# RWKV delta rule in chunks: the triangular inverse applied to strict keys and values ahead of the recursion

## The chip, the cores and the metric

The kernel runs on one core of one Trainium2 chip. The metric is the device time of one execution in microseconds, and the kernel before has a median of 2791.34 us of three runs (2788.96 to 2798.7). All data are fp32; the large matrices are multiplied as split fp32r parts, the small products of the recursion as plain fp32.

## The reference, cut to what matters

The model has two parts: first two hybrid layers (a mixer and an FFN each) on the tokens, then a second block with differential attention and an RWKV branch, both on the same tokens, followed by a PEER mixture of experts. The change is in the RWKV branch. It is a delta rule with decay, run over 256 tokens and 16 heads of 64, forward and over the reversed sequence (axis d):

```python
def wkv_scan(s0, scan_in):
    def step(s, inp):
        w, kk, a, k, v, r = inp
        sa = jnp.einsum('dbhij,dbhj->dbhi', s, kk)
        s = s * w[..., None, :] - sa[..., :, None] * (kk * a)[..., None, :] + v[..., :, None] * k[..., None, :]
        return s, jnp.einsum('dbhij,dbhj->dbhi', s, r)
    return lax.scan(step, s0, scan_in)
...
    s_ctx, y_c = wkv_scan(s0, scan_c)
    _, y_x = wkv_scan(s_ctx, scan_x)
```

It is scanned over the context first (only the state `s_ctx` is wanted), then over x from that state, where the outputs `y` are wanted.

## The kernel before

The scan is cut into 8 chunks of 32 tokens. Within a chunk the delta rule is solved by a 32 x 32 triangular inverse, so that the recursion has 8 steps of matrix products. Heads go in two halves (`hf`) of 8, in 4 tiles of two heads (index m, head b of the pair on partitions 64b to 64b+63). That makes four passes of `wkv_front` (line 1177) and `wkv_back` (line 1354): passes 1 and 2 on the context (src = 0, halves 0 and 1), each issued from `ffn` of layer 0 and 1, and passes 3 and 4 on x (src = 1), issued from `second`. The two directions run together in each pass.

`wkv_front` loads keys and values, normalises, builds decayed keys KB (K and B parts side by side), the strict keys and, for src = 1, the decayed r in WR, and the decay PC of each chunk. Per chunk it multiplies KB by WR (line 1300) and masks: ML holds the strict products, NK the inclusive ones (src = 1). Of ML, the rows 32 to 63 and 96 to 127 go through DRAM (din, lines 1311 to 1316) into Bt; a loop of 31 steps on VectorE (lines 1320 to 1325, tiles X, tmp) forms the inverses, which return through DRAM (dout, lines 1327 to 1332) into ML. Beside that loop, keys are transposed (KT, line 1346) and U = strict times values is formed (line 1353), both per chunk pair and direction, and each copied from PSUM by ScalarE (line 268).

`wkv_back` does per step n, for both directions (chunk n forward, chunk 7 - n backward): product of WR with the state S (line 1376), four sums into U on 32 partitions each (line 1381, recorded as line 274), for src = 1 four copies of the r part into Y, the inverse times U (line 1392) with two copies (line 268), the product with the keys (line 1404), and per direction S + product (line 274) and times the decay PC (line 271). For src = 1 the outputs follow (line 1420) and after them norm, bonus and gate, with a store to od (line 1453).

The Tile scheduler writes the order of each engine's queue before the run; the scan's work has a raised priority, and is woven into the work around it: FFN matmuls in passes 1 and 2, the projections of the second block and its attention in passes 3 and 4. In `ffn` the scan's matmuls have two PSUM banks (shown as m and x) that are taken in turn. In `second` the front has two and the back three. Tiles of 4 KB per partition come from a pool of tag w4 (5 slots in `ffn`, 8 in `second`), those of 8 KB from w8 (6 and 9 slots). A tile waits until the slot that it takes has been let go by its last reader. In pass 4, WR lies in the work tiles hh and hl. The state goes from `ffn` to `second` through DRAM (Sd, line 907).

## Time and profile before

| what | value |
|---|---|
| median of three runs | 2791.34 us (2788.96, 2791.34, 2798.7) |
| profiled execution, its own time | 2798.71 us |
| its span | 2796.9 us |
| TensorE busy | 2635.9 us (94%) |
| VectorE busy | 1978.4 us (71%) |
| ScalarE busy | 1423.3 us (51%) |
| GpSimd busy | 14.2 us, 45 instructions |

Times of the trace count from the span's start. PE is TensorE (PEld its weight load), DVE VectorE, ACT ScalarE, POOL GpSimd, SP the engine that issues DMAs. Tiles are named by the program: w stands for the pools w4 and w8, a, m, x for PSUM banks. A plain fp32 matmul is recorded as two instructions, a transpose against the identity as one. Passes 1 and 2 lie at about 390 to 667 and 1017 to 1263 us, passes 3 and 4 between 1355 and 1835 us; the experts follow.

### The profile page before, as it was taken

What the parts mean: (1) busy time and instruction counts of PE and PEld (TensorE: products, weight loads), DVE (VectorE), ACT (ScalarE), POOL (GpSimd) and SP (SyncE); (2) the same over time, 40 slices, a digit from 0 to 9 for tenths busy, and PEclk for the clock granted to TensorE, in tenths of its full rate; (3) what the DMA queues carried; (4) which work ended last, traced back from release to release, by engine and by line L of the source; (5) the groups of instructions that cost most, each with busy time, mean ns of one, the idle gap of its engine ahead of it and who ended that gap; (6) DMA issues with size and microseconds to landing.
All of it is one profiled execution on the core that took longest, in us unless ns stands there. A gap on an engine that the chain in (4) does not pass through costs nothing.

```text
span 2796.9 us, 54976 instructions
## 1 busy us (share of the span) xinstructions
PE 2635.9 (94%) x21856; PEld 2293.4 (82%) x21856; DVE 1978.4 (71%) x4085; ACT 1423.3 (51%) x2392; POOL 14.2 (1%) x45
## 2 busy tenths in 40 slices
PE   7999899999999999987998979989989999999999
PEld 7986588886997768877888755779989998888887
DVE  5996668765897658766788776566987765666665
ACT  4554446543555446534664655444446554444444
POOL 0000000000000000000000000000000000000000
PEclk9999999999999999988999976699999999999999
DMA  5532866546543555535746522264664346666665
GB/s 189 175 124 88 263 225 199 168 152 219 167 147 126 162 199 170 173 107 166 237 134 200 166 68 59 67 200 163 190 185 137 122 149 208 215 208 219 207 216 183
DMA packets 212433, 472.00 MB, mean 169 GB/s; under 512 B 52816, under 2 KB 86480, under 8 KB 211152
## 3 DMA queue, kind: packets, MB, share of 16 engines
q1 hardware_dynamic: 212176, 468.48, 52.4%
q8 instruction: 172, 2.82, 0.4%
q14 instruction: 85, 0.70, 0.1%
HBM read 427.77 MB, written 40.63 MB: 167 GB/s over the span
## 4 chain that ended last, share of the span: by engine, by line
PE 79%; DVE 10%; DMA 6%; ACT 4%; issue 2%; SPq 0%; DVEq 0%; ACTq 0%
PE a L333 8%; PE a L335 8%; PE a L334 8%; PE b L353 4%; PE b L351 4%; PE b L352 4%; PE b L1767 3%; PE x L335 3%; PE x L333 3%; PE x L334 3%; PE a L352 3%; PE a L351 3%; PE a L353 3%; DVE wl L277 3%; DMA raw<-in_peer 2%
## 5 line engine op out<-in xcount | busy, mean ns | idle before, releaser
L312 ACT ACTIVATE wh<-raw 128x1024 fp32r<-128x1024 f32 (+1 forms) x701 | 638.2, 913 | 689.3 <-PE a L334 247.4
L277 DVE TENSOR_TENSOR wl<-raw,wh 128x1024 fp32r<-128x1024 f32 (+1 forms) x701 | 727.4, 1041 | 357.9 <-ACT wh L312 332.6
L333 PE MATMUL a<-hh,wh 128*128 128x256 f32 x1920 | 550.2, 287 | 8.8 <-ACT hh L1621 4.1
L335 PE MATMUL a<-hh,wl 128*128 128x256 f32 x1920 | 549.5, 286 | 4.5 <-DVE wl L277 4.2
L334 PE MATMUL a<-hl,wh 128*128 128x256 f32 x1920 | 547.2, 285 | 0.6 <-DVE hl L277 0.5
L333 PEld LDWEIGHTS a<-hh,wh 128*128 128x128 f32 x1920 | 365.5, 190 | 22.0 <-ACT wh L312 4.9
L335 PEld LDWEIGHTS a<-hh,wl 128*128 128x128 f32 x1920 | 365.2, 190 | 14.8 <-DVE wl L277 9.0
L334 PEld LDWEIGHTS a<-hl,wh 128*128 128x128 f32 x1920 | 364.9, 190 | 5.4 <-DVE hl L277 0.7
L333 PE MATMUL x<-hh,wh 128*128 128x256 f32 x720 | 205.8, 286 | 5.6 <-ACT wh L312 5.2
L335 PE MATMUL x<-hh,wl 128*128 128x256 f32 x720 | 206.6, 287 | 3.0 <-DVE wl L277 3.0
L334 PE MATMUL x<-hl,wh 128*128 128x256 f32 x720 | 204.9, 285 | 0.0
L352 PE MATMUL b<-wl,ah 128*128 128x512 f32 x512 | 201.0, 393 | 0.0
L351 PE MATMUL b<-wh,ah 128*128 128x512 f32 x512 | 191.2, 393 | 2.8 <-issue 2.8
L353 PE MATMUL b<-wh,al 128*128 128x512 f32 x512 | 191.8, 391 | 0.0
L333 PEld LDWEIGHTS x<-hh,wh 128*128 128x128 f32 x720 | 137.2, 191 | 9.0 <-ACT wh L312 6.7
L335 PEld LDWEIGHTS x<-hh,wl 128*128 128x128 f32 x720 | 136.9, 190 | 5.7 <-DVE wl L277 4.4
L1802 ACT ACTIVATE ah<-pact 128x256 fp32r<-128x256 f32 x128 | 52.6, 412 | 173.1 <-PE b L352 160.3
L334 PEld LDWEIGHTS x<-hl,wh 128*128 128x128 f32 x720 | 137.1, 190 | 0.8
L352 PE MATMUL a<-wl,hh 128*128 128x256 f32 (+2 forms) x416 | 128.6, 309 | 8.0 <-DVE wl L277 7.9
L351 PE MATMUL a<-wh,hh 128*128 128x256 f32 (+2 forms) x416 | 125.3, 308 | 6.2 <-DVE hl L395 3.9
L277 DVE TENSOR_TENSOR wl<-rawv,wh 128x1024 fp32r<-128x1024 f32 x84 | 101.7, 1222 | 37.1 <-ACT wh L312 37.0
L353 PE MATMUL a<-wh,hl 128*128 128x256 f32 (+2 forms) x416 | 125.9, 304 | 0.0
(672 smaller groups left out, 5436.7 us busy)
## 6 DMA issues: line engine op xcount, KB each, us to landing
raw<-in_flat SPq DMA_DIRECT2D x289, 512.0 KB, 4.0
raw<-in_peer SPq DMA_DIRECT2D x172, 512.0 KB, 3.9
raw<-in_flat SPq DMA_DIRECT2D x228, 256.0 KB, 3.6
rawv<-in_peer SPq DMA_DIRECT2D x84, 512.0 KB, 4.6
TG<-in_flat SPq DMA_DIRECT2D x52, 512.0 KB, 5.9
parked<-act SPq DMA_DIRECT2D x89, 128.0 KB, 2.1
pact<-parked SPq DMA_DIRECT2D x89, 128.0 KB, 4.5
w<-vtd SPq DMA_DIRECT2D x32, 128.0 KB, 4.1
```

What stands on the lines that cost most here:

```text
L277: self.nc.vector.tensor_tensor(out, a, b, op=ALU.subtract)
L312: self.nc.scalar.activation(h, src, AF.Copy)
L333: mm(ps, wh[:, k], xh[:, k], start=first and k == 0, stop=False)
L334: mm(ps, wh[:, k], xl[:, k], start=False, stop=False)
L335: mm(ps, wl[:, k], xh[:, k], start=False, stop=last and k == nk - 1)
L351: mm(ps, xh[:, k], wh[:, k], start=first and k == 0, stop=False)
L352: mm(ps, xh[:, k], wl[:, k], start=False, stop=False)
L353: self.last = mm(ps, xl[:, k], wh[:, k], start=False, stop=last and k == nk - 1)
L1767: nc.tensor.matmul(ps[:, c], a[:, n, g, :, c], b[:, g, :, c], start=n == 0, stop=n == 2)
L1802: nc.scalar.activation(ah, act, AF.Copy)
```

## The change

1. S is not cleared at first; in step 0 of a context pass the product with S is left out, and the key product is copied to S.
2. U tiles hold both directions by step: `UV[n % 2][:, n // 2]`. Values are loaded by 16 DMAs of half the size.
3. The strict keys in WR are transposed into four new w4 tiles AT: for src = 0 by 64 products with the identity and 16 copies, for src = 1 by 32 transposes and 8 copies.
4. U = strict times values, and then the inverse times U, are two passes of eight groups each ahead of the recursion (`half in (0, 32)`), apart from the key transposes.
5. alpha, the inverse applied to the strict keys, is formed (128 products, one group of banks per direction), multiplied by the decay of the chunk before and written over the strict keys in WR. For src = 1 GpSimd multiplies the r part likewise.
6. In the recursion, the inverse product with its copies is gone; the sums into U are two masked ones over 128 partitions (`urows`); D = S times decay is formed by GpSimd beside the S product, and S = D + key product. The context passes multiply S by the last decay at the end.

```diff
@@ -902,8 +902,7 @@
             wa = tg[:, :T]
             nc.sync.dma_start(wa, self.wad)
             S = self.t(pool, [128, 2, 4, 64], "S")
-            nc.gpsimd.memset(S, 0.0)
-            self.wkv_back(self.wkv_front(pool, 0, l, self.zc, wa), S)
+            self.wkv_back(pool, self.wkv_front(pool, 0, l, self.zc, wa), S)
             nc.sync.dma_start(self.Sd[l], S)
...
@@ -1304,6 +1303,12 @@
                     if src:
                         self.mul(NK[:, d, q, b], pq[b][:, d, :, 0], incl[:, d].unsqueeze(1).to_broadcast([128, 4, 32]))
+        if src:
+            for d in range(2):
+                now, old = slice(1 - d, 8 - d), slice(d, 7 + d)
+                v = WR[d][:, :, now, 0]
+                nc.gpsimd.tensor_tensor(v, v, PC[:, d, :, old].unsqueeze(3).to_broadcast([128, 4, 7, 32]), op=ALU.mult)
...
@@ -1333,11 +1338,13 @@
         KT = [k.rearrange("p m (q c) x s -> p m q (c x s)", c=2) for k in KB]
-        UV = [self.w8(pool, [128, 4, 4, 128]) for d in range(2)]
-        for d in range(2):
-            for g in range(4):
-                o = UV[d].rearrange("p (t h) m c -> p h t (m c)", h=2)
-                nc.sync.dma_start(o[64 * (g % 2):64 * (g % 2) + 32, g // 2], vtd[32 * g:32 * g + 32])
+        UV = [self.w8(pool, [128, 4, 4, 128]) for e in range(2)]
+        for g in range(4):
+            rows, at = slice(64 * (g % 2), 64 * (g % 2) + 32), slice(32 * g, 32 * g + 32)
+            for t in range(2):
+                for d in range(2):
+                    n = 4 * t + g if d == 0 else 7 - 4 * t - g
+                    nc.sync.dma_start(UV[n % 2][rows, n // 2].rearrange("p m c -> p (m c)"), vtd[at, t])
         for q in range(4):
             for d in range(2):
                 qd = q if d == 0 else 3 - q
@@ -1345,67 +1352,111 @@
                 for m in range(4):
                     nc.tensor.transpose(ps[:, m], KT[d][:, m, qd], self.ident)
                 self.evac(KT[d][:, :, qd], ps)
+        AT = [[self.w4(pool, [128, 2, 4, 128]) for h in range(2)] for d in range(2)]
+        for q in range(4):
+            for d in range(2):
+                at = AT[d][q // 2][:, q % 2]
+                ps = self.bank().rearrange("p (m c) -> p m c", m=4)
+                for m in range(4):
+                    if src:
+                        nc.tensor.transpose(ps[:, m], WR[d][:, m, 2 * q:2 * q + 2].rearrange("p c x s -> p (c x s)"), self.ident)
+                        continue
+                    for c2 in range(2):
+                        mm(ps[64 * c2 + 32:64 * c2 + 64, m], WR[d][:, m, 2 * q + c2, 0], self.ident, start=True, stop=True)
+                if src:
+                    self.evac(at, ps)
+                else:
+                    for c2 in range(2):
+                        u = slice(64 * c2 + 32, 64 * c2 + 64)
+                        self.evac(at[u], ps[u])
+        steps = lambda n: [(d, *divmod(n if d == 0 else 7 - n, 2)) for d in range(2)]
+        for half in (0, 32):
+            for n in range(8):
+                uv = UV[n % 2][:, n // 2]
                 ps = self.bank().rearrange("p (m b i) -> p m b i", m=4, b=2)
                 for m in range(4):
                     for b in range(2):
-                        for c2 in range(2):
-                            R = slice(64 * c2, 64 * c2 + 32)
-                            mm(ps[64 * c2 + 32:64 * c2 + 64, m, b], ML[R, d, qd, b, m], UV[d][R, qd, m, 64 * b:64 * b + 64], start=True, stop=True)
+                        for d, q, c2 in steps(n):
+                            R = slice(64 * c2 + half, 64 * c2 + half + 32)
+                            mm(ps[64 * c2 + 32:64 * c2 + 64, m, b], ML[R, d, q, b, m], uv[R, m, 64 * b:64 * b + 64], start=True, stop=True)
                 for c2 in range(2):
                     u = slice(64 * c2 + 32, 64 * c2 + 64)
-                    self.evac(UV[d][u, qd], ps[u].rearrange("p m b i -> p m (b i)"))
+                    self.evac(uv[u], ps[u].rearrange("p m b i -> p m (b i)"))
+        for d in range(2):
+            pa = [self.bank().rearrange("p (q m s) -> p q m s", q=4, m=4) for c2 in range(2)]
+            for q in range(4):
+                for m in range(4):
+                    for b in range(2):
+                        for c2 in range(2):
+                            u = slice(64 * c2 + 32, 64 * c2 + 64)
+                            mm(pa[c2][64 * b:64 * b + 64, q, m], AT[d][q // 2][u, q % 2, m, 64 * b:64 * b + 64], ML[u, d, q, b, m], start=True, stop=True)
+            for c2 in range(2):
+                al = WR[d][:, :, c2::2, src].rearrange("p m q s -> p q m s")
+                first = 0 if d == 0 else 7
+                if first % 2 != c2:
+                    lo, hi = 0, 4
+                else:
+                    lo, hi = 1 - d, 4 - d
+                    nc.vector.tensor_copy(al[:, first // 2], pa[c2][:, first // 2])
+                old = PC[:, d, :, 2 * lo + c2 + 2 * d - 1:2 * hi + c2 + 2 * d - 2:2].rearrange("p m q -> p q m")
+                self.mul(al[:, lo:hi], pa[c2][:, lo:hi], old.unsqueeze(3).to_broadcast([128, hi - lo, 4, 32]))
         Y = [self.w4(pool, [128, 2, 4, 128]) for d in range(2)] if src else None
-        return src, hf, PC, WR, KT, UV, ML, NK, Y, bond if src else None
-    def wkv_back(self, state, S, od=None):
-        src, hf, PC, WR, KT, UV, ML, NK, Y, bond = state
+        W = [w.rearrange("p m c x s -> p (m c x s)") for w in WR] if src else wc.rearrange("p d m c s -> p (d m c s)")
+        return src, hf, PC, W, KT, UV, NK, Y, bond if src else None
+    def wkv_back(self, pool, state, S, od=None):
+        src, hf, PC, W, KT, UV, NK, Y, bond = state
         nc, P = self.nc, self.P2
         mm = nc.tensor.matmul
         m0 = 4 * hf
-        U64 = [u.rearrange("p q m (b i) -> p q m b i", b=2) for u in UV]
+        U64 = [UV[n % 2][:, n // 2].rearrange("p m (b i) -> p m b i", b=2) for n in range(8)]
         for n in range(8):
             dc = [(d, *divmod(n if d == 0 else 7 - n, 2)) for d in range(2)]
-            pp = [self.bank()[:, 0:256].rearrange("p (m i) -> p m i", m=4) for b in range(2)]
-            for m in range(4):
-                for d, q, c2 in dc:
-                    rows = slice(64 * c2, 64 * c2 + 64) if src else slice(64 * c2 + 32, 64 * c2 + 64)
-                    for b in range(2):
-                        Q = slice(64 * b, 64 * b + 64)
-                        mm(pp[b][rows, m], WR[d][Q, m, 2 * q + c2].rearrange("p x s -> p (x s)"), S[Q, d, m], start=True, stop=True)
-            for d, q, c2 in dc:
-                u = slice(64 * c2 + 32, 64 * c2 + 64)
+            if src or n:
+                pp = [self.bank()[:, 0:256].rearrange("p (m i) -> p m i", m=4) for b in range(2)]
+                for m in range(4):
+                    for d, q, c2 in dc:
+                        c = 8 * m + 2 * q + c2
+                        w, c = (W[d], 64 * c) if src else (W, 1024 * d + 32 * c - 32)
+                        for b in range(2):
+                            Q = slice(64 * b, 64 * b + 64)
+                            mm(pp[b][64 * c2:64 * c2 + 64, m], w[Q, c:c + 64], S[Q, d, m], start=True, stop=True)
                 for b in range(2):
-                    self.add(U64[d][u, q, :, b], U64[d][u, q, :, b], pp[b][u])
+                    nc.vector.scalar_tensor_tensor(U64[n][:, :, b], pp[b], self.urows, U64[n][:, :, b], op0=ALU.mult, op1=ALU.add)
+            if n:
+                D = self.t(pool, [128, 2, 4, 64], "D" if src else "wup", bufs=1)
+                for d in range(2):
+                    c = n - 1 if d == 0 else 8 - n
+                    nc.gpsimd.tensor_tensor(D[:, d], S[:, d], PC[:, d, :, c].unsqueeze(2).to_broadcast([128, 4, 64]), op=ALU.mult)
             if src:
                 for d, q, c2 in dc:
                     t, g = divmod(2 * q + c2, 4)
                     yv = Y[d][32 * g:32 * g + 32, t].rearrange("p m (b i) -> p b m i", b=2)
                     for b in range(2):
                         nc.scalar.activation(yv[:, b], pp[b][64 * c2:64 * c2 + 32], AF.Copy)
-            pt = self.bank().rearrange("p (m b i) -> p m b i", m=4, b=2)
-            for m in range(4):
-                for b in range(2):
+                if n == 7:
+                    break
+            pk = [self.bank()[:, 0:256].rearrange("p (m i) -> p m i", m=4) for d in range(2)]
+            for b in range(2):
+                Q = slice(64 * b, 64 * b + 64)
+                for m in range(4):
                     for d, q, c2 in dc:
-                        u = slice(64 * c2 + 32, 64 * c2 + 64)
-                        mm(pt[u, m, b], ML[u, d, q, b, m], U64[d][u, q, m, b], start=True, stop=True)
-            for d, q, c2 in dc:
-                u = slice(64 * c2 + 32, 64 * c2 + 64)
-                self.evac(UV[d][u, q], pt[u].rearrange("p m b i -> p m (b i)"))
-            if src and n == 7:
-                break
-            pk = [self.bank()[:, 0:256].rearrange("p (m i) -> p m i", m=4) for d in range(2)]
-            for m in range(4):
-                for d, q, c2 in dc:
-                    R = slice(64 * c2, 64 * c2 + 64)
-                    for b in range(2):
-                        Q = slice(64 * b, 64 * b + 64)
-                        mm(pk[d][Q, m], KT[d][R, m, q, Q], U64[d][R, q, m, b], start=True, stop=True)
-            for d, q, c2 in dc:
-                self.add(S[:, d], S[:, d], pk[d])
-                self.mul(S[:, d], S[:, d], PC[:, d, :, 2 * q + c2].unsqueeze(2).to_broadcast([128, 4, 64]))
+                        R = slice(64 * c2, 64 * c2 + 64)
+                        mm(pk[d][Q, m], KT[d][R, m, q, Q], U64[n][R, m, b], start=True, stop=True)
+            for d in range(2):
+                if n or src:
+                    self.add(S[:, d], D[:, d] if n else S[:, d], pk[d])
+                else:
+                    nc.vector.tensor_copy(S[:, d], pk[d])
         if not src:
+            for d in range(2):
+                self.mul(S[:, d], S[:, d], PC[:, d, :, 7 - 7 * d].unsqueeze(2).to_broadcast([128, 4, 64]))
             return
         yf = Y[0]
...
@@ -1557,6 +1608,10 @@
         self.kcol = self.t(pool, [128, 2], "kcol")
...
+        self.urows = self.t(pool, [128, 1], "urows")
+        nc.gpsimd.memset(self.urows, 0.0)
+        for c2 in range(2):
+            nc.gpsimd.memset(self.urows[64 * c2 + 32:64 * c2 + 64], 1.0)
...
```

## Rows read from the trace of the kernel before

**Rows 1.** Chain of work that ended last, page: share of the span by engine.

```profile
PE 79%; DVE 10%; DMA 6%; ACT 4%; issue 2%; SPq 0%; DVEq 0%; ACTq 0%
```

**Rows 2.** Stretches: length, busy PE, PEld, DVE, ACT, POOL, PE clock, DMA share, GB/s.

```profile
510.00:600.00 90.00, 90.00 (x869) 78.67 (x868) 62.82 (x95) 41.53 (x50) 0.00 (x0) 1.00 0.53 171
...
1140.00:1234.50 94.50, 94.37 (x900) 80.93 (x898) 64.11 (x100) 42.93 (x54) 0.00 (x0) 1.00 0.54 163
1234.50:1262.70 28.20, 18.25 (x354) 14.94 (x352) 15.20 (x53) 7.23 (x14) 0.00 (x0) 0.61 0.09 38
...
1690.00:1800.00 110.00, 100.57 (x954) 69.30 (x957) 60.84 (x156) 55.76 (x150) 0.00 (x0) 0.57 0.18 50
```

**Rows 3.** Pass 1, lines 1353, 1376, 1392, 1207, 1300: busy PE, PEld, clock.

```profile
390.00:667.00 277.00, 8.66 (x256) 7.37 (x256) 1.00 0.54 173
...
390.00:667.00 277.00, 6.99 (x256) 4.89 (x256) 1.00 0.54 173
...
390.00:667.00 277.00, 8.95 (x256) 7.49 (x256) 1.00 0.54 173
...
390.00:667.00 277.00, 1.97 (x32) 1.73 (x32) 1.00 0.54 173
...
390.00:667.00 277.00, 4.76 (x256) 4.21 (x256) 1.00 0.54 173
```

**Rows 4.** Chain of waits, end of pass 2: start us, us, engine, tile, line.

```profile
1249.27 1.96 PE x L1392 x32
...
1251.25 0.60 ACT w L268
...
1251.89 0.90 PE m L1404 x12
...
1253.06 0.43 DVE S L274
...
1253.51 0.44 DVE S L271
...
1254.09 0.39 PE m L1376 x2
...
1255.90 0.75 DVE w L274 x2
...
1257.24 1.95 PE m L1392 x32
...
1262.72 1.98 DMA Sd<-S
```

**Rows 5.** Pass 2, lines 1353 and 1392: min/median/max ns, first and last start.

```profile
L1353 PE MATMUL m<-w,w x256: 214/214/238, 1097.7 to 1137.2; 32*32 32x64 f32 x128
...
L1392 PE MATMUL x<-w,w x128: 214/214/309, 1163.2 to 1250.9; 32*32 32x64 f32 x128
```

**Rows 6.** Timeline of PE, two steps under the FFN: start us, us.

```profile
1185.48 1.08 PE L1392 MATMUL m<-w,w 32*32 32x64 f32 x32
...
1200.67 1.08 PE L1392 MATMUL x<-w,w 32*32 32x64 f32 x32
```

**Rows 7.** Timeline of DVE, pass 4's second B product.

```profile
1622.26 1.23 DVE L1281 SCALAR_TENSOR_TENSOR w<-w,w 128x1024 f32<-128x1024 f32 x1 [0.91 <-PE a L1404]
```

**Rows 8.** Pass 4, line 1392, 1690 to 1800 us, as rows 5.

```profile
L1392 PE MATMUL a<-w,w x256: 214/309/312, 1706.9 to 1793.8; 32*32 32x64 f32 x128
```

**Rows 9.** Chain of waits, end of the attention and pass 4's store.

```profile
1771.35 0.38 ACT xn L1501
...
1826.15 5.15 DMA od<-w
```

**Rows 10.** Timeline of PE, pass 2, line 1300, both banks.

```profile
1063.48 0.66 PE L1300 MATMUL x<-w,w 64*64 64x32 f32 x16
...
1078.64 0.25 PE L1300 MATMUL x<-w,w 64*64 64x32 f32 x2
```

**Rows 11.** Groups of POOL: mean ns behind the busy time.

```profile
L642 POOL COPY P<-zk 128x256 f32<-128x256 f32 x4 | 2.0, 520 | 75.6 <-ACT zk L268 75.6
```

More of the change, by code (lines that the diff above doesn't have):

```diff
@@ L1235, in wkv_front @@
         else:
-            wr = self.w8(pool, [128, 2, 4, 8, 32])
-            WR = [wr[:, d].unsqueeze(3) for d in range(2)]
+            wc = self.w8(pool, [128, 2, 4, 8, 32])
+            WR = [wc[:, d].unsqueeze(3) for d in range(2)]
         PC = self.t(pool, [128, 2, 4, 8], "PC", bufs=2)
@@ L1419, in wkv_back @@
                             R = slice(64 * c2, 64 * c2 + 64)
-                            mm(ps[32 * g:32 * g + 32, m, b], NK[R, d, q, b, m], U64[d][R, q, m, b], start=d == 0, stop=d == 1)
+                            mm(ps[32 * g:32 * g + 32, m, b], NK[R, d, q, b, m], U64[4 * t + g if d == 0 else 7 - 4 * t - g][R, m, b], start=d == 0, stop=d == 1)
             self.add(yf[:, t], yf[:, t], Y[1][:, t])
@@ L1582, in back @@
             with self.stream("r"), self.tc.high_priority(offset=30000):
-                self.wkv_back(state, S, od)
+                self.wkv_back(pool, state, S, od)
         def front(*args):
```

## The prediction, made before the changed kernel was run

> **What bounds the kernel now.** I read the chain of waits first: TensorE holds 79% of the way to the end [rows 1]. So the question for every edit is whether TensorE has room where the edit falls. The stretch view answers it by stage. In both FFN stretches there is none: 90.00 of 90 us and 94.37 of 94.5 us are busy [rows 2]. There the recursion is filler: it costs TensorE time, not latency. After the second FFN's last matmul the opposite holds: from 1234.5 to 1262.7 us TensorE is busy for 18.25 of 28.20 us at clock 0.61 [rows 2]; only the end of pass 2 runs, one engine at a time [rows 4], and the second block waits for the state that is stored at 1262.72. Pass 4 lies beside the attention, TensorE being busy for 100.57 of 110 us at clock 0.57 [rows 2]; its recursion outlives the attention, which ends near 1771 [rows 9]. Pass 3 lies inside the projections and the early attention. So there are four places: pass 1 (TensorE work alone counts), the end of pass 2 (latency alone counts), pass 3 (nearly free), pass 4 (latency, bounded by the attention's end).
>
> **Part 1: TensorE work in pass 1.** Plain matmuls are recorded as two instructions each. Removed: the eight inverse products of the recursion, 8.95 us [rows 3], and, as the first step has no state yet, one of eight S products, 6.99/8 = 0.87 us [rows 3]. Added: the inverse on U ahead of the recursion, as many products of the same shape as the old strict pass, 8.66 us by that row, 8.95 by the removed one [rows 3]; I take 8.95, so that this is a move. Added: alpha, 128 calls, 256 records, nearest to the row of 256 records with 32 columns, 4.76 us; the upper end is the 8.95 us of the 32-deep row [rows 3]. Added: the transposed strict keys, 64 calls against the identity, 128 records. The nearest row is the other product against the identity, 1.97 us for 32 records, 0.062 each, so 7.9 us; as that has 64 weight columns and these have 32, the lower end is the price per record of the 4.76 us row, 2.4 us, and the upper end twice the value taken, 15.8 us [rows 3]. Sum: 7.9 + 8.95 + 4.76 - 8.95 - 0.87 = 11.8, taken as **+12** (bounds +6 to +24). Since TensorE is full, nothing hides it. Pass 2 pays the same, but ends at another bound, below. The dropped memset of S, the mask constant and the doubled number of value loads (16 of half the size) go at nothing: the loads are wanted only after the keys' transposes, and if that cover fails they cost one load's latency per pass.
>
> **Part 2: the end of pass 2.** Alone, a step now takes 1257.24 - 1249.27 = 7.97 us [rows 4]: inverse product 1.96, copy out 0.60 with its gap 0.64, product with the keys to its sum 1.17, sum 0.43, decay 0.44, then the S product from 1254.09 to 1255.90 (1.81 with its gap), and the four sums till 1257.24 (1.34). The new step drops the inverse and its copy (1.97 + 0.64) and the decay (0.44), and has two masked sums of 128 rows for four of 32: two by 0.43 of the same 256 columns and a gap of 0.14, 1.0 for 1.34. That is 7.97 - 1.97 - 0.64 - 0.44 - 0.34 = 4.6; I take 4.7. GpSimd's product of decay and state (D) has the S product, the masked sums and the key product as its cover, 1.81 + 1.0 + 1.17 = 4.0 us.
>
> How many such steps are left over? Under the FFN a step costs visits to a full queue: 1200.67 - 1185.48 = 15.2 us for three visits [rows 6]; with two I take 10. But the recursion starts later. It starts now when the inverse lands, at 1163.2 [rows 5]. In the new order the inverse goes onto U in eight groups first, then alpha. The old strict pass, interleaved with the key transposes, ran sixteen groups between 1097.7 and 1137.2 [rows 5], 2.5 us each; so eight groups take 20 us and alpha's four some 8 (between 2 and 2.5 each): start at 1191. The FFN's last matmul, at 1234.5, moves by the added work of this pass. I take 12 more, and 2.5 for products which the FFN used to cover for being behind it: 1249. By then 58/10 = 5.8 steps are done, before 3.5 of 8 were left; 2.2 are left, 2.2 x 4.7 = 10.3, and the last decay 0.9: the store starts at 1260 against 1262.7, **-2**. Bounds: if the start comes at 1180 (the strict pass's 64 records need little when matmuls alone pace them) all but one step is covered and the store comes near 1251, -12; if the steps keep 12 us and the start 1200, 4.1 are done, 3.9 are left, 1249 + 19 = 1268 and some 2 for the transposed keys, +8.
>
> **Part 3: passes 3 and 4.** The keys, alpha and U cost TensorE some 4 us more in each pass, by the sum above with transposes for matmuls; in pass 3 there is room for most of it. In pass 4 a wait falls away: the second direction's B product could start only at 1622.26, when pass 3's last key product had freed its slot [rows 7]. The new code lets go of the slot of the inverse after alpha, before the recursion. I give the front **-9**, after 4 us of its own new work, since next the attention's vector work and the same DVE queue are late; bounds 0 and -20. From the inverse's first product at 1706.9 to the last at 1793.8 [rows 8] are 87 us, with the tail 88. New: 28 us for U and alpha as above, and eight steps. Each had 88/8 = 11 us with three visits among the attention's matmuls; two thirds are 7.3, and the decay off the chain makes it 6.7: 54. 28 + 54 = 82, **-6**. But what lies behind cannot come before the attention, 1771, and the other branch's merge; from there the result's store at 1826.15 follows [rows 9]. So of -15 I take **-11** (bounds -20 and +10).
>
> The GpSimd products are shown by no row: the trace has one GpSimd copy of 128 x 256 at 0.52 us [rows 11]. At that price D is 1.04 us for both directions, below the 4.0 us of cover, and the product over seven chunks (896 columns, twice in passes 3 and 4) 2 x 1.8 us beside the inverse. From both sides: 0 while covered, as VectorE only gives work away; and with products four times as long as the copy D fills its cover, and each further microsecond is one per step. I take 0. The Trainium skill, "GPSIMD Engine Reference", sections 1 and 3.1, speaks against the move: it gives some 2.6 cycles per element for a GpSimd sum or product of two tensors, by which 256 elements take an estimated 0.6 us, and says that GpSimd shares its way to SBUF with VectorE's operations of two inputs. By it D would still fit its cover, and the sum would move towards R3's time. No run shown here has a GpSimd operation with two inputs, so the trace neither agrees nor differs.
>
> **The sum** against the profiled execution (2798.71 us, 7.36 above the median of 2791.34): +12 - 2 - 11 = -1, 2797.7, or **2790** on the median's scale.
>
> **Rivals.** Measurement can tell about 0.3%, 8.4 us, from no change.
> F, the sum: TensorE pays in pass 1 what latency gains later. Own range 2780 to 2800. Chance 0.38.
> R1, faster: the early start of U is not paced by banks but by matmuls, so the tail of pass 2 is covered, and pass 4's gate opens wholly. Pass 1 at +9, pass 2 at -12, passes 3 and 4 at -20: -23, **2768**. For it: a 7.97 us step is all latency [rows 4]; against it: pass 4 has the attention beside it. Chance 0.27.
> R2, slower: transposed keys take four slots of a pool that has five in the FFN, of which the inverse holds three while it runs. The third key tile then waits for the inverse's end, its matmuls filling the bank that its copy can't empty. The two banks of this stream are taken in turn, and one that is held does stop the other: in pass 2 sixteen products stand filled at 1063.48 and the rest of that group comes at 1078.64 [rows 10]. The strict pass, which before ran beside the inverse, then starts when it ends: 8 x 2.5 = 20 us more of latency in passes 1 and 2. Pass 1 at +12 (its end is hidden by FFN work), pass 2 at +8, passes 3 and 4 at +8, where the same pool is short by Y: +28, **2819**. It decides as soon as the third key tile finds no free slot before the inverse ends. Chance 0.25.
> R3, slower: D holds up the sums on the chain. If VectorE waits for one GpSimd operation of the copy's 0.52 us [rows 11] at each of the 32 products that no FFN covers (4 at the end of pass 2, 14 each in passes 3 and 4), that is 17 us on top of the sum: **2807**. It decides when D takes more than the 4.0 us of its cover, or when the two engines do not run beside one another. Chance 0.10.
>
> **How the numbers follow.** Faster by over 0.3%: R1 and a quarter of F's lower end, 0.27 + 0.09 = 0.36. Slower: R2, nearly all of R3's 0.10 and a little of F: 0.33. The rest, 0.31, is no change. The signs are balanced, so the range goes from R1's time to just past R2's, 2768 to 2822; below lies R1's better half (0.13), above it R2's worse tail (0.07).
>
> **What would show it.** Right: more TensorE time in 390 to 667 by some 12 us with FFN1 as much later; a step in the tail near 4.7 us; the store of the state within 5 us of 1262.7; pass 4's B product before 1620, and its recursion in steps below 8 us. R1 shows as an FFN end with under 1.5 steps left; R2 as copies of the key tiles that wait for a slot until the inverse's last DVE step, with the strict pass behind them; R3 as sums of S released by GpSimd. Wrong would be above all a large fall or rise in a stage that I count as full, or the attention itself moved by the copies that passes 3 and 4 put on ScalarE.

## The result, and the profile after

The changed kernel takes 2873.11 us (median of four, 2864.48 to 2881.15) against 2790.15 us for the kernel before: a ratio of 1.0293, 95% interval 1.0254 to 1.0331, some 82 us slower. The forecast was 2790 us, the range ended at 2822.

Busy time by engine, from the page of the changed kernel:

```profile
span 2872.2 us, 57632 instructions
...
PE 2672.7 (93%) x23136; PEld 2344.7 (82%) x23136; DVE 1945.2 (68%) x3985; ACT 1447.4 (50%) x2440; POOL 57.4 (2%) x112
```

TensorE is busy for 37 us more in the whole span, VectorE for 33 us less, and the span is 75 us longer. So half of the loss at least is waiting: TensorE stands idle for 38 us more. The stretches (columns as in [rows 2]): two in the FFNs, the end of pass 2, the stretch after pass 4's strict products.

```profile
510.00:600.00 90.00, 89.95 (x1033) 79.64 (x1033) 48.98 (x66) 58.98 (x82) 0.00 (x0) 1.00 0.51 160
1150.00:1250.00 100.00, 98.19 (x1095) 87.40 (x1094) 54.51 (x74) 63.90 (x87) 0.00 (x0) 1.00 0.48 150
1264.00:1300.60 36.60, 26.27 (x481) 22.95 (x480) 16.96 (x50) 2.06 (x5) 8.39 (x14) 0.55 0.08 30
1700.00:1780.00 80.00, 60.23 (x542) 40.37 (x542) 56.50 (x152) 33.88 (x87) 4.24 (x3) 0.79 0.32 85
```

The stretch that runs alone at the end of pass 2 is 36.6 us long where it was 28.2 [rows 2], at a clock of 0.55: all eight steps of the recursion lie in it, not three and a half.

Where the time is lost, by places that both traces have (start of a step, us; traces differ by up to 5 us before pass 1, so differences between runs count from the first line):

| place | before | after | keys free (e1) | strict first (e2) | early keys (e3) |
|---|---|---|---|---|---|
| pass 1, first strict product | 435.4 | 435.6 | 430.2 | 430.3 | 431.9 |
| pass 2, keys loaded | 936.0 | 958.3 | 940.8 | 940.0 | 947.8 |
| pass 2, state stored | 1262.7 | 1300.6 | 1279.2 | 1271.8 | 1273.0 |
| pass 3, last key product ends | 1622.8 | 1690.9 | 1635.9 | 1631.1 | 1627.2 |
| pass 4, result stored | 1826.1 | 1891.8 | 1838.8 | 1840.8 | 1854.6 |
| end of span | 2796.9 | 2872.2 | 2823.0 | 2820.7 | 2829.5 |

Of the 75 us of the spans, 22 are lost by the start of pass 2, 16 more by its store, 30 more by the end of pass 3's recursion. From there to pass 4's store nothing more is lost, and 10 come in the unchanged stages behind (971 us in the trace before; in the traces of the other runs they take 968 to 984).

What happens in pass 3 is the key to it. TensorE's timeline of the changed kernel, transposed strict keys (line 1363) and the first group of strict times values (line 1383); then ScalarE's copies of the keys:

```profile
1495.95 0.60 PE L1363 MATMUL a<-ident,w 128*128 128x128 f32 x4
1497.20 0.60 PE L1363 MATMUL a<-ident,w 128*128 128x128 f32 x4
...
1555.07 1.04 PE L1363 MATMUL a<-ident,w 128*128 128x128 f32 x8
1559.01 1.04 PE L1363 MATMUL a<-ident,w 128*128 128x128 f32 x8
1562.48 1.04 PE L1363 MATMUL a<-ident,w 128*128 128x128 f32 x8
1564.22 1.98 PE L1383 MATMUL a<-w,w 32*32 32x64 f32 x64 [0.70 <-ACT w L268]
```
```profile
1552.35 1.08 ACT L268 ACTIVATE w<-a 128x512 f32<-128x512 f32 x2
```

Two groups are transposed and fill both banks of the front; their copies come 55 us later, right after the inverse's end (its store to DRAM is issued at 1549.8). Strict times values, which needs no inverse, then starts at 1564 behind them. In the FFN passes it is the same: products at 488, copies from 530.9, strict times values from 557.

But the slots were not full, as my rival R2 had it. Each tile has an address in the built program; set beside the trace, five of pass 3's eight w4 slots (0 to 7 by address) read, in us:

```
slot   last use before     next tile, first write
0      1458.6              key tile   1552.4
6      1459.7              key tile   1552.8
4      1461.7              key tile   1559.7
3      1491.2              key tile   1560.1
5      1455.1              TB         1553.9
```

Five of eight slots stand empty for 69 to 99 us. What the key tiles wait for stands ahead of them in the text: TB, of the same pool, which is first written when the inverse has come back. The copies at 1552.35 wait for no engine when they run: their row has no idle time, they follow straight on ScalarE's work before them. It is their place in ScalarE's queue, written before the run, that is late.

### The profile page after: what moved, and what is told of

Its sections match the earlier page's. It is cut to its first block, busy times and chain, and to the rows that moved or that the text cites. A ratio compares the mean times of both kernels' runs of the same rounds, so it can differ in the third digit from the quotient of the medians.

```text
span 2872.2 us, 57632 instructions
## 1 busy us (share of the span) xinstructions
PE 2672.7 (93%) x23136; PEld 2344.7 (82%) x23136; DVE 1945.2 (68%) x3985; ACT 1447.4 (50%) x2440; POOL 57.4 (2%) x112
## 5 line engine op out<-in xcount | busy, mean ns | idle before, releaser
L334 PEld LDWEIGHTS a<-hl,wh 128*128 128x128 f32 x1928 | 370.7, 192 | 6.5 <-issue 2.3
```

What stands on the lines that cost most here:

```text
L334: mm(ps, wh[:, k], xl[:, k], start=False, stop=False)
```

## The experiments

Ratios are against the kernel before, with 95% intervals; differences in us are the ratio times 2790. The changed kernel is at +82.

**e1: TB takes no slot.**

```diff
-        TB = self.w4(pool, [128, 32, 32])
+        TB = tmp.rearrange("p (k s) -> p k s", s=32)
```


> One line of the changed kernel: TB, the tile through which the inverse returns, no longer asks for a w4 slot but lies in tmp, which the inverse has done with. Theory O (slots are given in the order of the program text): in the changed kernel the key tiles AT stand behind TB in that order, and TB is first written when the inverse is done, so the copies of the keys wait for the inverse although slots are free (in pass 3 they come at 1552.4 us, and five of eight slots are free from 1488 on). By it, passes 3 and 4 copy all keys and form strict times values beside the inverse: pass 3's last key product comes some 20 us earlier (8 groups of 2.5 to 5 us), pass 4's store too; in the FFN only two slots are free beside the inverse, the third key tile still waits, so passes 1 and 2 gain 0 to 8 us. Time 20 to 40 us below the changed kernel, 2833 to 2853. Theory S (the slots are full, as I predicted): no change in passes 3 and 4, time within 8 us of 2873.

Measured 2823.42 us, 1.0134 (1.0109 to 1.0158), +37: one line gives back 45 of 82 us. In pass 3 all keys and strict times values now lie beside the inverse:

```profile
1473.85 0.60 PE L1363 MATMUL a<-ident,w 128*128 128x128 f32 x4
...
1484.41 1.03 PE L1363 MATMUL a<-ident,w 128*128 128x128 f32 x8
1486.97 1.98 PE L1383 MATMUL a<-w,w 32*32 32x64 f32 x64
```

Theory O holds for passes 3 and 4, theory S falls there. The gain is larger than expected, since the FFN passes gained too (pass 2's keys are loaded 12 us earlier at an equal start).

**e2: strict times values ahead of the keys.**

```diff
+        u_pass(0)
         AT = [[self.w4(pool, [128, 2, 4, 128]) for h in range(2)] for d in range(2)]
...
-        for half in (0, 32):
+        u_pass(32)
```
(`u_pass(half)` is the body of that loop. In e8 below, `u_group(half, n)` is one of its eight groups.)

> The changed kernel with the transposed keys moved behind the first of the two U passes (strict times values), all else the same. Theories O and S both: strict times values needs no key tile, so in all four passes it runs beside the inverse again, whatever makes the keys wait; the keys come behind it and still wait for the inverse. Eight groups of 2.5 us leave the chain of each pass: the state's store of pass 2 at 1278 to 1285 us in place of 1300.6, pass 4's store at 1850 to 1860 in place of 1891.8, time 30 to 45 us below the changed kernel. Rival W (what costs is the added TensorE work, wherever it stands): within 8 us of the changed kernel.

Measured 2822.44 us, 1.0143 (1.0106 to 1.018), +40. Another edit, which leaves the slots as they are, gives back the same: what costs is that strict times values stands behind the waiting keys. The state's store came at 1271.8 and pass 4's at 1840.8 in a trace that began 5 us earlier, so both a little ahead of what was expected. Rival W falls.

**e3: no key tile waits, in the FFN either.** TB as in e1, and

```diff
-        AT = [[self.w4(pool, [128, 2, 4, 128]) for h in range(2)] for d in range(2)]
+        if src:
+            AT = [[self.w4(pool, [128, 2, 4, 128]) for h in range(2)] for d in range(2)]
+        else:
+            lp = self.t(pool, [128, 32, 33], "lp", bufs=1).rearrange("p c s -> p (c s)")[:, 0:1024]
+            free = [lp, self.t(pool, [128, D], "TG", bufs=4)]
+            AT = [[self.w4(pool, [128, 2, 4, 128]), f.rearrange("p (q m c) -> p q m c", q=2, m=4)] for f in free]
```


> The changed kernel with TB in tmp, and in the FFN two of the four key tiles in slots of other pools that are done with (the one of the decay sums, and one of the FFN's own ring of four). Now no key tile should wait for the inverse in any pass. Theories O and S: recursion of pass 2 starts at about 1190 (inverse) + 22 + 9 = 1221 us in place of 1264, so that some 3 of its steps run under the FFN; state's store at about 1275 to 1280; passes 3 and 4 as in the run with TB alone; time 45 to 65 us below the changed kernel, 2808 to 2828, still above the kernel before since pass 1 pays 17 us and pass 4 waits for pass 3's last key product. Rival W: within 15 us of the changed kernel.

Measured 2834.83 us, 1.0177 (1.0147 to 1.0207), +49: a miss, more than e1. In pass 2 it did what it should: from keys loaded to state stored 325.2 us, against 326.7 before and 342.3 in the changed kernel. That looks like the -2 that I had forecast, but pass 2 with the old code took 323.0 to 325.5 in e5, e7, e10 and e11, so a gain over the old code is not shown. The time is lost in the second block: 581.6 us from that store to pass 4's, against 563.4 before and 559.6 in e1, whose code it has there. The rows of the inverse on U and of alpha in pass 2 (line 1388 and line 1400; min/median/max ns, first and last start):

```profile
L1388 PE MATMUL x<-w,w x128: 214/214/238, 1171.7 to 1197.1; 32*32 32x64 f32 x128
...
L1400 PE MATMUL m<-w,w x64: 217/218/238, 1197.3 to 1207.5; 32*64 32x32 f32 x64
```

The eight groups take 25.6 us and alpha 11.4, so 37 us together. (The 48 us of the expectation of e8, below, take in the last groups of strict times values.)

**e4: D on VectorE.** `nc.gpsimd.tensor_tensor(D[:, d], ...)` becomes `nc.vector.tensor_tensor(D[:, d], ...)`.

> The changed kernel with D, the state times the decay, formed by VectorE in place of GpSimd. Rival G (the GpSimd products hold the chain up): the time falls by 10 to 20 us, and the steps at the end of pass 2, 4.4 us now, become shorter. Theories O and S: the step gets two products of 0.42 us on VectorE, of which only a part lies beside the S product, so steps become the same or up to 0.8 us longer; time from no change to 15 us above the changed kernel.

Measured 2866.22 us, 1.0286 (1.0264 to 1.0309), +80: no difference that counts. Rival G, my R3, falls.

**e5, e6, e7: the change in pass 1, in pass 2, in passes 3 and 4 alone.**

```diff
-            self.wkv_back(pool, self.wkv_front(pool, 0, l, self.zc, wa), S)
+            if l + 1 in NEW:
+                self.wkv_back(pool, self.wkv_front(pool, 0, l, self.zc, wa), S)
+            else:
+                nc.gpsimd.memset(S, 0.0)
+                self.wkv_back_o(pool, self.wkv_front_o(pool, 0, l, self.zc, wa), S)
```
(NEW is (1,), (2,) or (3, 4); the functions with `_o` are those of the kernel before.)

> The change as it is in pass 1 alone (context, first half of the heads, in the first FFN); passes 2, 3 and 4 as before. Theory O (slot order) with the TensorE work of my forecast: the FFN is full, so the pass costs its added TensorE work, 10 to 12 us as in the runs where the keys are early, and 4 to 8 us more because keys, U and recursion all come after the inverse and the last steps outlive the FFN: 14 to 20 us above the kernel before, 2802 to 2808. Rival W (the loss is added work all over): a quarter of the whole loss, 20 us, too; then the runs with the change in the other passes must show 20 and 40.

> The change as it is in pass 2 alone. Theory O: the state's store comes 13 to 20 us later than in the kernel before (TensorE's added work 12, and a recursion that starts only after the FFN's end, 8 steps of 4.4 us alone, against 3.5 steps of 8 us); the second block follows one for one, as it waits for the state: 13 to 20 us above the kernel before, 2801 to 2808. If the second block hides it (its first work could run from other data), 0 to 5 us.

> The change as it is in passes 3 and 4 alone; both context passes as before. Theory O: pass 3's last key product comes 30 us later, since strict times values, alpha and all of the recursion follow the inverse; pass 4's strict products take a slot that this key product frees, and come 30 us later as well; the store of the result 28 to 35 us later, time 30 to 45 us above the kernel before, 2818 to 2832. The three runs together should give the 83 us of the whole change within 15 us. If pass 4 does not hang on pass 3, its own front (which starts 94 us later in the changed kernel) shows 60 us or more; if the attention hides both, under 10.

Measured: pass 1 alone 1.0115 (1.01 to 1.013), +32; pass 2 alone 1.0123 (1.0108 to 1.0138), +34; passes 3 and 4 alone 1.011 (1.0091 to 1.013), +31. The sum is 97, 15 more than the whole. In the first two the traces come near the expectations up to the state's store (+17 and +21, counted from an equal start) but 13 and 18 us more are lost behind it, where the code is that of the kernel before. That was new: the scheduler lays out all queues from one simulated timeline, and a change in pass 1 gives the second block another order. The traces bear this out: VectorE's instructions of the second block stand in another order than in the kernel before, in e5 and e6 as in e9, e10 and e13 below. With passes 3 and 4 alone, pass 3's last key product comes 28 us later, as expected, but the result's store only 16, a miss (that trace is 8 us below the median of its runs).

**e8: the inverse on U inside the recursion.** e3 with alpha first, one group of the inverse on U ahead of the recursion and the next one in each step:

```diff
+        u_group(32, 0)
...
+            if n < 7:
+                u_group(32, n + 1)
             pk = [self.bank()[:, 0:256].rearrange("p (m i) -> p m i", m=4) for d in range(2)]
```


> The version with early keys in all passes, and with the second U pass cut up: alpha comes first after the inverse, then the inverse on U of step 0, and that of each later step stands in the recursion behind the sums of the step before it, beside its key product. Same work. Theory: in the run with early keys the eight groups and alpha took 1161 to 1209 us, 48 us where I had put 28, as each group waits for its turn among the FFN's matmuls; now only alpha and one group stand between the inverse and the recursion. Pass 2's recursion then starts near 1180 and lies almost wholly under the FFN, the state's store at 1250 to 1262; pass 3's end 15 to 20 us earlier than with early keys. Time 20 to 40 us below the run with early keys, 2795 to 2815. Rival: the groups' places in TensorE's queue cost the same wherever they stand, and the time stays within 8 us of 2834.

Measured 2838.09 us, 1.0174 (1.0151 to 1.0197), +49, as e3: a miss, and the rival holds. The recursion starts earlier in pass 2, its first key product at 1194.3 for 1211.3 in e3, but the state is stored at 1281.5, no earlier.

**e9: useless work in the kernel before.**

```diff
+        for k in range(0 if src or hf else 6):
+            nc.vector.memset(tmp, 0.0)
         for k in range(31):
```


> The kernel before with six fillings of tmp (128 x 1024, some 0.5 to 1 us each on VectorE) ahead of the inverse in pass 1 alone: useless work beside a full FFN, of which VectorE has a third idle. It moves the inverse of pass 1 by 3 to 6 us and with it the scheduler's whole order of the queues after it, the attention's and pass 4's too, which has no other work than before. Theory R (a reordered second block costs by itself: in the runs with the change in pass 1 or pass 2 alone, 17 and 20 us were lost by the state's store, but 27 and 38 at the end): the time rises by 5 to 20 us though no engine that bounds has more work, and the loss lies behind the store of the state. Rival (the loss behind the store has to do with the change's own work): within 5 us of the kernel before.

Measured 2799.29 us, 1.0051 (1.0021 to 1.0081), +14. Up to the state's store its profiled execution is not behind that of the kernel before (1257.1 against 1262.7), and it ends 2 us earlier, so no trace shows where the 14 are lost; the medians differ by 9, and three of its twelve runs, at 2814 to 2827, make up the rest. The fillings take 0.91 us each on an engine with room. That the order of the queues costs the 14 is thus argued, not shown; if it does, it is worth as much as any term of my forecast.

**e10: the line of e1 in the kernel before.**

> The kernel before with the one line of the first run: TB in tmp. There it has no key tiles behind it. What it reorders lies in passes 3 and 4 alone. Theory O: TB held up nothing that mattered, as only Y comes behind it: the context passes unchanged; passes 3 and 4 within 5 us but for reordering, which theory R puts at 0 to 15 us. If the line gains by itself (20 us or more), then the 50 us of the first run were not those of the waiting keys.

Measured 2804.03 us, 1.0044 (1.0029 to 1.006), +12: no gain by itself. So the 45 us of e1 are put down to the waiting keys, to within the 12 to 15 us that an edit can move by the order alone; e2 gives 42 by another way.

**e11: the transposed keys of pass 1 as dead work in the kernel before.**

```diff
+        if not src and not hf:
...
+                            mm(ps[64 * c2 + 32:64 * c2 + 64, m], WR[d][:, m, 2 * q + c2, 0], self.ident, start=True, stop=True)
```


> The kernel before with the 64 products against the identity of pass 1 added, into PSUM banks, their results not used. It prices the transposed keys on a full TensorE alone: my forecast had 7.9 us (2.4 to 15.8). The state's store of pass 1 and the start of pass 2 come 5 to 9 us later; at the end 5 to 9 by theory W, 10 to 28 with the reordering of theory R.

Measured 2810.63 us, 1.0075 (1.0048 to 1.0101), +21: the work, 7.98 us by its row, and 13 more that fit the reordering of e9 and e10. Of the two places named, pass 1's state is stored 3 us later and pass 2 starts 13 us later, both outside 5 to 9.

**e12, e13, e14: the change without its core**, in all passes, in both context passes, in pass 2 alone. The inverse is applied in the recursion as before; what is left is U by step, masked sums, D on GpSimd, no first S product, and GpSimd puts the decay on the strict keys:

```diff
+            v = WR[d][:, :, now].rearrange("p m c x s -> p m c (x s)")
+            nc.gpsimd.tensor_tensor(v, v, PC[:, d, :, old].unsqueeze(3).to_broadcast([128, 4, 7, 32 * (1 + src)]), op=ALU.mult)
```


> The change without its core: no key tiles, no alpha, the inverse stays in the recursion; the rest is kept (U tiles by step for both directions, 16 value loads, no S product in step 0 of the context, two masked sums for four, D on GpSimd with S = D + product, the decay put on the strict keys by GpSimd ahead of the recursion). TensorE's work falls by the S product of step 0 alone. Theory O with R: a step at the end of pass 2 takes 8.0 - 0.44 - 0.34 = 7.2 us for 8.0, some 3 us less there, 5 us less in passes 3 and 4; with the reordering -8 to +12 us against the kernel before. If these parts cost by themselves (GpSimd's products over the keys ahead of the recursion, the doubled loads): 15 us or more.

> The parts of the change without its core (as in the run before: U by step, masked sums, D on GpSimd, no first S product) in both context passes; passes 3 and 4 as in the kernel before. In the run with these parts in all passes the state's store of pass 2 came 12 us earlier at an equal start (1245.4 against 1262.7, of which 5 had been gained before the first pass), and all of it was lost in passes 3 and 4. Theory R: 12 us gained, less 12 to 15 for another order of the second block: -5 to +5 us against the kernel before. If the loss was that of the parts in passes 3 and 4 themselves: 8 to 15 us faster than the kernel before.

> The same parts in pass 2 alone, where the steps after the FFN's end run alone. 2.5 to 3 us are to be had from shorter steps (7.2 for 8.0 us) at the state's store, and the order of the second block is another: 0 to +14 us against the kernel before by theory R; -3 without it.

Measured: 1.0054 (1.0036 to 1.0073), +15; 1.0043 (1.0027 to 1.0059), +12; 1.0014 (0.9999 to 1.003), +4. These parts shorten the context passes: the state is stored at 1245.4 and 1251.0 where the first strict product was at 430.4 and 429.3, so 12 and 6 us earlier than before at an equal start. All of it and more is lost in the second block, also in e13, whose second block has the old code. No version beats the kernel before.

**e15: the useless work of e9 in the changed kernel.**

> The changed kernel with the same useless fillings in pass 1 that moved the kernel before by about 14 us. They ask what the order of the queues is worth around the changed kernel. If its 83 us hold a share that is only an unlucky order, the time moves by 5 to 15 us, down as well as up; theory O says that 50 us of the 83 stay whatever the order, so it stays above 2850. In the kernel before the same fillings could only lose if its order is a good one by choice.

Measured 2875.42 us, 1.0293 (1.027 to 1.0317): nothing moves. The same nudge costs the kernel before 14 us. Four of five edits to the kernel before that should have been neutral or better (e9, e10, e12, e13) cost 12 to 15 us, the fifth (e14) 4: the order of its queues seems to be a good one that hardly any neighbour has. Which exchange in the order costs this is not shown; the profiled execution of the kernel before was itself 8.7 us above the median of its runs here, so single traces cannot place 13 us.

## Why the prediction was wrong, step by step

**Part 1, TensorE's work in pass 1: right.** The rows of the changed kernel for lines 1366 (keys), 1383 (both U passes), 1395 (alpha), 1429 (S product), 1451 (key product), 1353 (key transposes), as in [rows 3]:

```profile
390.00:690.00 300.00, 7.96 (x128) 6.62 (x128) 1.00 0.52 165
...
390.00:690.00 300.00, 15.80 (x512) 14.51 (x512) 1.00 0.52 165
...
390.00:690.00 300.00, 4.26 (x256) 4.04 (x256) 1.00 0.52 165
...
390.00:690.00 300.00, 6.14 (x224) 4.63 (x224) 1.00 0.52 165
...
390.00:690.00 300.00, 8.29 (x256) 7.19 (x256) 1.00 0.52 165
...
390.00:690.00 300.00, 4.29 (x32) 3.64 (x32) 1.00 0.52 165
```

The keys cost 7.96 (forecast 7.9), alpha 4.26 (4.76). With the key product and the key transposes of the kernel before,

```profile
390.00:667.00 277.00, 5.59 (x256) 4.49 (x256) 1.00 0.54 173
...
390.00:667.00 277.00, 5.08 (x32) 3.55 (x32) 1.00 0.54 173
```

the six lines sum to 46.7 us, against 35.3 before: +11.5 for +12. Part of that closeness is luck: the forecast's own terms come to 9.6, as the two U passes take 15.80 for 17.61 where I had a move, and the key product, not foreseen, adds 2.7 (8.29 for 5.59 with the same records). In the kernel before consecutive key products stepped through both halves of rows and of columns; with b outermost they keep one half of the columns. That this is the cause is argued: under the FFN the 32 records of a step take 0.69 or 0.70 us in the old order (the kernel before, e9, e14) and 0.97 or 0.98 in the new one (the changed kernel, e1, e12, e15), but the layout of U changed with the order in all of these. Pass 2's start came 22 us later: pass 1's state is stored 17 us later (683.5 for 666.5, counted from an equal start), as its recursion outlived the FFN by 5, and 5 more are lost behind it. In e1, where the last key of pass 1 is transposed at 531 in place of 552, pass 2 starts only 10 us later.

**Part 2, the end of pass 2: the step right, the start wrong.** GpSimd's timeline of the changed kernel shows the cadence of the steps, by their D:

```profile
1266.43 1.20 POOL L1436 TENSOR_TENSOR wup<-S,PC 128x256 f32<-128x256 f32 x2 [174.89 <-DVE S L1456]
1271.71 1.20 POOL L1436 TENSOR_TENSOR wup<-S,PC 128x256 f32<-128x256 f32 x2 [4.08 <-DVE S L274]
1276.41 1.20 POOL L1436 TENSOR_TENSOR wup<-S,PC 128x256 f32<-128x256 f32 x2 [3.51 <-DVE S L274]
1281.12 1.20 POOL L1436 TENSOR_TENSOR wup<-S,PC 128x256 f32<-128x256 f32 x2 [3.50 <-DVE S L274]
```

That is 4.70 us a step; I had 4.7. But I let the recursion start at 1191 and 5.8 steps pass under the FFN. It started at 1264, so that all steps ran alone, 36.6 us of tail for the 11 that I had. The sentence that failed is "eight groups take 20 us and alpha's four some 8": it took for granted that the other eight groups stay beside the inverse. In the changed kernel both U passes come after it:

```profile
L1383 PE MATMUL x<-w,w x256: 214/214/238, 1204.2 to 1246.3; 32*32 32x64 f32 x128
...
L1395 PE MATMUL x<-w,w x128: 217/218/238, 1252.5 to 1261.2; 32*64 32x32 f32 x128
```

Sixteen groups from 1204 to 1247, 2.7 us each, alpha 8.9 us: both prices were near, eight groups too few were counted. With the keys early (e3) the eight groups took 3.2 us each and alpha 11.4, and the rest came as forecast: steps of 9 to 11 us under the FFN (I took 10), two to three left at its end at 1258.1 (2.2).

**Part 3, passes 3 and 4: wrong.** The step that failed here is "pass 3 (nearly free)". From the state's store to pass 3's last key product it takes 390.3 us for 360.1; with the keys free 356.7 (e1), with strict times values first 359.3 (e2). So the 30 us lost there are those of strict times values behind the waiting keys. In pass 4 I gave -9 for a gate that falls away. It did: the inverse's slot is free at 1608.4. The next tile has the same gate. ML of pass 4 takes the slot of pass 3's keys KB, and is first written when the last product has read them (TensorE, then VectorE, changed kernel):

```profile
1689.38 1.54 PE L1451 MATMUL a<-w,w 64*64 64x64 f32 x32
```
```profile
1690.38 0.49 DVE L271 TENSOR_TENSOR w<-a,consts 128x128 f32<-128x128 f32 x2
```

So pass 4 hangs on pass 3's end as before, and that came 68 us later, of which 38 are passes 1 and 2. Also unseen: pass 4's front starts at 1612.4 for 1517.5, since its tiles stand behind pass 3's Y in the text, and Y is first written by the recursion's first step, which now needs alpha. From pass 4's inverse to its result's store it took 131.6 us (1760.2 to 1891.8) for 126.0 (1700.1 to 1826.1), not 6 less: here too all sixteen U groups follow the inverse. From pass 3's last key product to that store it is 200.9 for 203.3.

**The rivals.** R2 had the right event, keys waiting for the inverse with strict times values behind them, and too small a price: +28 for some 45, as I let the FFN hide it in pass 1 and let passes 3 and 4 pay 8 us. Its cause, full slots, is wrong for passes 3 and 4: e1 asks for one slot less, yet all four key tiles come early. In the FFN it is half right, as the inverse does hold three of the five slots. In e1, with TB out of the way, two key tiles of pass 1 are written at 483 and 484, the third only at 523, when the inverse lets go of a slot, and strict times values starts at 534; with other slots for the keys (e3) it starts at 510. What I read from [rows 10], that one bank held up the other, was wrong: the products of 1063.48 are the first direction's, they stand in both banks, and the rest waits for the second direction's keys, whose last product on VectorE ends at 1075.6. R3 fell with e4: D takes 1.2 us at the end of pass 2, in a cover of 4, and up to 3.2 in passes 3 and 4. R1's early start (1180, with under 1.5 steps left at the FFN's end) never came; nearest is e3, with its first key product at 1211 and two to three steps left.

**What was not priced at all** is the order of the queues, 12 to 15 us for four of five edits to the kernel before that should have been neutral or better. Of the 82 us, 45 are the waiting keys (e1, with e2 at 42); of the 37 left, 11.5 are TensorE's work in pass 1 by its rows. That some 13 more are the order is argued from e9 and e10 and not shown in the changed kernel, where the nudge of e15 moved nothing. So 12 us stay open with it, 25 without.

## What to carry to other kernels

Where a pool gives its slots in the order of the text, a tile waits for the first write of the tiles ahead of it even if slots are free: look what an added tile stands behind, and give a tile that is written late a place that asks for nothing. Where a gate falls, look for the next tile with the same gate before the gain is booked. Where one simulated timeline orders all queues, run an edit without effect beside the real one, and take what it costs as the floor under any forecast.

## What the runs showed of the hardware

A GpSimd product of two inputs of 128 x 256 takes 0.62 us at the end of pass 2, where it runs beside little else. In passes 3 and 4 the mean is 0.72. Groups of GpSimd in the changed kernel (busy, mean ns, idle before):

```profile
L1436 POOL TENSOR_TENSOR D<-S,PC 128x256 f32<-128x256 f32 x28 | 19.7, 722 | 341.9 <-DVE S L274 319.7 <-DVE sm L1529 22.1
L1436 POOL TENSOR_TENSOR wup<-S,PC 128x256 f32<-128x256 f32 x28 | 16.8, 622 | 423.4 <-DVE S L1456 348.6 <-DVE S L274 63.5 <-DVE sm L413 11.4
...
L1310 POOL TENSOR_TENSOR w<-w,PC 128x896 f32<-128x896 f32 x2 | 3.7, 1862 | 25.4 <-PE a L1299 25.4
```

The mean hides two cases. In passes 3 and 4, 24 of the 28 products take 0.62 us as well; four take 1.07 to 1.60, each while VectorE works on 512 or 1024 elements a row from two inputs in SBUF. VectorE is slowed by it too. The four products of GpSimd between 1685 and 1697 us, and the operation of VectorE beside two of them, in the whole trace and in that stretch (min/median/max ns, first and last start):

```profile
L1436 POOL TENSOR_TENSOR D<-S,PC x4: 620/844/1070, 1686.1 to 1694.4; 128x256 f32<-128x256 f32 x4
```
```profile
L1539 DVE SCALAR_TENSOR_TENSOR x<-x,sm x16: 739/750/1084, 1656.8 to 1804.8; 128x512 f32<-128x512 f32 x16
...
L1539 DVE SCALAR_TENSOR_TENSOR x<-x,sm x2: 1079/1082/1084, 1686.2 to 1693.9; 128x512 f32<-128x512 f32 x2
```

The Trainium skill, "GPSIMD Engine Reference", sections 1 and 3.1, lets expect an estimated 0.6 us for 256 elements a row and 2 us for 896; the trace agrees (0.62; 1.86). Its section 1 also says that GpSimd shares its interfaces to SBUF with VectorE and contends with VectorE's operations on two SBUF inputs; the trace agrees (1.07 us for 0.62, and 1.08 for 0.75 on VectorE). On the whole kernel this had no weight: moving D to VectorE changed nothing that can be measured (e4).

Beside the first FFN, at a granted clock of 1.00, the 32 records of a step's key product took 0.70 us in the kernel before and 0.98 us in the changed one. Their order among rows and columns, or the layout of U that came with it, is worth that much.
